# Masked softmax on one core: a contiguous first batch, the last masks moved, batch 14 stored in halves, the first store held longer

The kernel runs on one core of a Trainium2 chip. The metric is device microseconds (us) of that core. Executions are classed as fast or slow by their time and granted clock.

## The reference

For each of 16 batches (8 heads x 256 query rows = 2048 rows of 256 numbers, 2 MB in float32) the first `length` columns of each row go through a softmax; the others are zero.

```python
for b in range(batch):
    length = lengths[b]
    masked = x[b, :, :, :length].copy()
    masked = masked - np.max(masked, axis=-1, keepdims=True)
    exp_masked = np.exp(masked)
    result[b, :, :, :length] = exp_masked / np.sum(exp_masked, axis=-1, keepdims=True)
```

The lengths (128 to 255) are data. A load may stop a little past the length; all of the output must be written.

## The kernel before

A batch is 128 partitions x 16 rows. Eight slots in SBUF hold batches. SyncE loads batches 0 to 3 whole; GpSimd loads the other twelve, with rows cut to one of 11 widths or whole. VectorE masks (a minimum with a falling ramp), ScalarE takes exponentials with their sums half a batch at a time, VectorE divides by halves, and SyncE stores.

```python
x_f = x.rearrange("b h q k -> b (h q) k").rearrange("b (p t) k -> b p t k", p=P)
...
def parts(b):                       # the pieces in which a batch is stored
    if b == 0:
        cuts = [0, nt]
    elif b < 8:
        cuts = [0, half, half + quarter, nt]
    elif b < 13 or b == batch - 1:
        cuts = [0, half, nt]
    else:
        cuts = [0, nt]
...
for h in range(2):
    s = slice(h * half, (h + 1) * half)
    nc.sync.dma_start(out=xt[:, 0, s], in_=x_f[0, :, s]).then_inc(s_ld[h], 16)
for b in range(1, ahead):
    nc.sync.dma_start(out=xt[:, b], in_=x_f[b]).then_inc(s_ld[b + 1], 16)

nc.sync.wait_ge(s_exp, 3)           # the first store is held for three half tiles of ScalarE
for b in range(batch):
    s_b = s_st[b % 2]
    for s in parts(b):
        nc.sync.wait_ge(s_out, 2 * b + (s.stop - 1) // half + 1)
        if b >= 2 and s.start == 0:
            nc.sync.wait_ge(s_b, 64 * (b // 2 + 1))      # the store of batch b - 2 has landed
        nc.sync.dma_start(out=out_f[b, :, s, :], in_=xt[:, b % slots, s, :]).then_inc(s_b, ...)
...
for b in range(batch):              # VectorE
    first = b == 0 or b >= ahead
    if first:
        divide(b, 0)
    if b + 1 < batch:
        mask(b + 1, slice(0, nt))
    if not first:
        divide(b, 0)
    divide(b, 1)
...
with nc.Fori(0, 2 * batch, 1, engines=[ACT]) as i:
    nc.scalar.wait_ge(s_min, i + 1)
    for j in range(half):
        ins = nc.scalar.activation(out=e, in_=e, func=EXP, accum_out=...)
    ins.then_inc(s_exp, 1)
```

The softmax here doesn't subtract the row's maximum and nothing guards it: scores larger than these inputs give would overflow.

Of the kernel before, what the change touches and what calls it, by code (L numbers as in the profile page):

```python
# [20 lines left out]
def kernel(  # L21
# [6 lines left out]
    nc = tc.nc  # L28
    P = nc.NUM_PARTITIONS

    batch, heads, seq_q, seq_k = x.shape
    rows = heads * seq_q
    assert rows % P == 0
    nt = rows // P
    half = nt // 2
    quarter = nt // 4

    x_f = x.rearrange("b h q k -> b (h q) k").rearrange("b (p t) k -> b p t k", p=P)
    out_f = out.rearrange("b h q k -> b (h q) k").rearrange("b (p t) k -> b p t k", p=P)

    slots = 8
    ahead = 4
    assert slots - ahead == 4 and batch % slots == 0
# [6 lines left out]
    def parts(b):  # L50


        if b == 0:
            cuts = [0, nt]
        elif b < 8:
            cuts = [0, half, half + quarter, nt]
        elif b < 13 or b == batch - 1:
            cuts = [0, half, nt]
        else:
            cuts = [0, nt]  # L60
        return [slice(i, j) for i, j in zip(cuts, cuts[1:])]
# [3 lines left out]
    xt = pool.tile([P, slots, nt, seq_k], F32, name="xt")  # L65
# [13 lines left out]
    sem = lambda n: ctx.enter_context(nc.semaphore(n))  # L79
    s_st = [sem("s_st0"), sem("s_st1")]  # L80
    with tc.tile_critical(no_gpsimd_drain=True):  # L81
# [4 lines left out]
        s_ld = [sem(f"s_ld{k}") for k in range(ahead + 1)]  # L86
# [5 lines left out]
        s_v = sem("s_v")  # L92
        s_min = sem("s_min")
        s_exp = sem("s_exp")
        s_out = sem("s_out")

        def length(engine, at):

            return nc.values_load(  # L99
                at,  # L100
                engines=[engine],
                skip_runtime_bounds_check_because="compared with constants, never an address",
            )
# [2 lines left out]
        nc.scalar.dma_start(out=word64, in_=lengths[None, :]).then_inc(s_word, 16)  # L106
        for h in range(2):
            s = slice(h * half, (h + 1) * half)
            nc.sync.dma_start(out=xt[:, 0, s], in_=x_f[0, :, s]).then_inc(s_ld[h], 16)  # L109
        for b in range(1, ahead):  # L110
            nc.sync.dma_start(out=xt[:, b], in_=x_f[b]).then_inc(s_ld[b + 1], 16)  # L111

        nc.sync.wait_ge(s_exp, 3)
        for b in range(batch):
            s_b = s_st[b % 2]
            for s in parts(b):
                nc.sync.wait_ge(s_out, 2 * b + (s.stop - 1) // half + 1)
                if b >= 2 and s.start == 0:
                    nc.sync.wait_ge(s_b, 64 * (b // 2 + 1))
                nc.sync.dma_start(  # L120
                    out=out_f[b, :, s, :], in_=xt[:, b % slots, s, :]
                ).then_inc(s_b, 16 * ((s.stop - s.start) // quarter))



# [44 lines left out]
        def step(ins):  # L170
            nonlocal v
            v += 1
            ins.then_inc(s_v, 1)
# [5 lines left out]
                out=down, in0=iota_i, scalar1=0.5, scalar2=-big, op0=ALU.add, op1=ALU.mult  # L179
# [7 lines left out]
                out=len_s, in0=len_f, scalar1=big, scalar2=None, op0=ALU.mult  # L187
# [4 lines left out]
        def clip(b, s, lo, hi):  # L192

            t = xt[:, b % slots, s, lo:hi]
            return nc.vector.scalar_tensor_tensor(  # L195
                out=t,
                in0=down[:, None, lo:hi].to_broadcast([P, s.stop - s.start, hi - lo]),
                scalar=len_s[:, b : b + 1],
                in1=t,
                op0=ALU.add,  # L200
                op1=ALU.min,
            )

        def mask(b, s):
            v_len = length(DVE, word[0:1, 2 * b : 2 * b + 1])
            if b == 0:
                nc.vector.wait_ge(s_ld[s.start // half], 16)
            elif b < ahead:
                nc.vector.wait_ge(s_ld[b + 1], 16)
            else:  # L210
                nc.vector.wait_ge(s_sw[b % 2], 16 * ((b - ahead) // 2 + 1))
            with nc.vector.If(v_len < mid):  # L212
                clip(b, s, 0, mid)
            clip(b, s, mid, seq_k).then_inc(s_min, (s.stop - s.start) // half)

        def divide(b, h):
            s = slice(h * half, (h + 1) * half)
            nc.vector.wait_ge(s_exp, 2 * b + h + 1)
            step(nc.vector.reciprocal(out=inv_sum[:, b, s], in_=row_sum[:, b, s]))  # L219
            nc.vector.wait_ge(s_v, v)  # L220
            t = xt[:, b % slots, s, :]
            nc.vector.tensor_tensor(  # L222
                out=t,
                in0=t,
                in1=inv_sum[:, b, s, None].to_broadcast([P, half, seq_k]),
                op=ALU.mult,
            ).then_inc(s_out, 1)
# [3 lines left out]
        for b in range(batch):  # L231


            first = b == 0 or b >= ahead
            if first:
                divide(b, 0)
            if b + 1 < batch:
                mask(b + 1, slice(0, nt))
            if not first:
                divide(b, 0)  # L240
            divide(b, 1)


        nc.scalar.activation(out=warm, in_=nc.const_aps.tensor(0.0, (P, 1), F32), func=EXP)  # L244
# [2 lines left out]
        with nc.Fori(0, 2 * batch, 1, engines=[ACT]) as i:  # L247
            nc.scalar.wait_ge(s_min, i + 1)
            at = bass.ds(i % (2 * slots), 1)
            for j in range(half):  # L250
                e = x_h[:, at, j, :]
                ins = nc.scalar.activation(  # L252
                    out=e, in_=e, func=EXP, accum_out=sum_h[:, bass.ds(i, 1), j]
                )
            ins.then_inc(s_exp, 1)


# [33 lines left out]
```

## Time and profile before

| before | value |
|---|---|
| time, median of 6 runs | 156.53 us (155.87 to 156.64) |
| span of the profiled run | 154.7 us |
| VectorE, ScalarE, GpSimd busy | 75%, 68%, 12% |
| DMA | 62.06 MB to and from HBM, 401 GB/s over the span |

A kernel that moves 62 MB at a plateau of some 430 GB/s needs 144 us for that alone. So read the profile for the stretches in which the DMA runs below the plateau. (A packet, below, is what the profile records as one move of a DMA engine, here mostly 4 to 16 KB.) The prediction shows those of the start, of the hand-over from loads to stores, and of the end. What it doesn't show is how the first two loads, the halves of batch 0, landed (the last line of the view of the line that issues them: microseconds from issue to last landing; with two loads, the least is the first half's, the greatest the second's and the median their mean):

```profile
DMA to landing us min/median/max: 5.2/6.2/7.2
```

When the last store was issued (SyncE's timeline: start, length):

```profile
146.65 0.36 SPq L120 DMA_DIRECT2D out_dram<-xt  x1
```

Last, the chain that ended last, by engine:

```profile
DMA 55%; DVE 19%; ACT 8%; issue 8%; ACTq 2%; SPq 1%; POOLq 1%; DVEq 0%
```

The chain ends in VectorE's divides and the last store.

### The profile page before, as it was taken

To read this page: it belongs to the slowest core of one execution; us is meant where nothing else is said; L and a number is where in the kernel's file an instruction comes from. 1 tells how busy PE (TensorE), PEld (TensorE's weight loads), DVE (VectorE), ACT (ScalarE), POOL (GpSimd) and SP (SyncE) were. 2 spreads that over 40 slices of the span, in tenths; PEclk is the share of its full clock that TensorE was granted. 3 is DMA by queue.
4 is the path that set the end of the run, shared out by engine and by line. 5 is a ranking of instruction groups with operands and counts; after the bars stand their busy time and mean duration, and the time that the engine had idled before them with its cause. 6 is when DMAs were issued, how large, how long until landed. Compare 5 with 4: busy or idle time off the path is not lost.

```text
span 154.7 us, 1324 instructions
## 1 busy us (share of the span) xinstructions
PE 0.2 (0%) x1; PEld 0.1 (0%) x1; DVE 115.7 (75%) x84; ACT 105.2 (68%) x514; POOL 19.0 (12%) x25
## 2 busy tenths in 40 slices
PE   0000000000000000000000000000000000000000
PEld 0000000000000000000000000000000000000000
DVE  1249999952999696979979696969689629796700
ACT  3087799992692959778695959595976906959200
POOL 4910031000220110201111020202001000000000
DMA  4999999999999999999999999999999999999992
GB/s 116 426 449 424 428 398 406 398 407 447 400 410 395 402 409 414 415 417 411 404 424 407 417 408 409 415 416 416 416 417 419 419 448 415 426 445 419 430 421 85
DMA packets 9988, 62.08 MB, mean 401 GB/s; under 512 B 850, under 2 KB 946, under 8 KB 6274
## 3 DMA queue, kind: packets, MB, share of 16 engines
q1 hardware_dynamic: 5904, 41.95, 65.8%
q0 software_dynamic: 4080, 20.12, 32.1%
q14 instruction: 2, 0.02, 0.0%
q10 hardware_dynamic: 2, 0.00, 0.0%
HBM read 28.51 MB, written 33.55 MB: 401 GB/s over the span
## 4 chain that ended last, share of the span: by engine, by line
DMA 55%; DVE 19%; ACT 8%; issue 8%; ACTq 2%; SPq 1%; POOLq 1%; DVEq 0%
DMA xt<-in_x_dram 34%; DMA out_dram<-xt 21%; DVE xt L222 9%; DVE xt L195 9%; ACT xt L252 8%; ACTq L252 2%; DVE inv_sum L219 1%; SPq L109 1%; POOLq L99 0%; SPq L111 0%; SPq L120 0%; DVEq L212 0%; POOLq L135 0%; POOLq L130 0%; ACTq L247 0%
## 5 line engine op out<-in xcount | busy, mean ns | idle before, releaser
L252 ACT ACTIVATE xt<-xt x256 | 102.4, 401 | 37.2 <-DVE xt L195 37.2
L222 DVE TENSOR_TENSOR xt<-xt,inv_sum 128x2048 f32<-128x2048 f32 x32 | 73.4, 2292 | 1.1
L252 ACT ACTIVATION_READ_ACCUMULATOR xt<-xt x256 | 47.9, 187 | 0.0
L195 DVE SCALAR_TENSOR_TENSOR xt<-down,len_s,xt 128x2048 f32<-128x2048 f32 (+1 forms) x17 | 37.8, 2222 | 13.1 <-DMA xt<-in_x_dram 13.0
L130 POOL DMA_DIRECT2D xt<-in_x_dram x12 | 12.8, 1064 | 95.5 <-issue 50.6
L219 DVE RECIPROCAL inv_sum<-row_sum 128x8 f32<-128x8 f32 x32 | 6.3, 198 | 14.4 <-ACT xt L252 14.4
L149 POOL MEMSET xt<- 128x1536 f32 x4 | 5.3, 1386 | 1.1 <-DVE len_s L186 1.1
L244 ACT ACT_TABLE_LOAD x1 | 1.3, 1283 | 1.6 <-SPq L81 1.6
L178 DVE TENSOR_SCALAR down<-iota_i 128x256 f32<-128x256 int32 x1 | 0.3, 297 | 1.6 <-POOL iota_i L141 1.6
L183 DVE CAST len_b<-word 1x16 bf16<-1x16 int32 x1 | 0.2, 163 | 0.4 <-DMA word<-in_lengths_dram 0.4
L186 DVE TENSOR_SCALAR len_s<-len_f 128x16 f32<-128x16 f32 x1 | 0.2, 174 | 0.3 <-PE len_f L165 0.3
L141 POOL IOTA iota_i<- 128x256 int32 x1 | 0.3, 331 | 0.6 <-SPq L81 0.6
L146 POOL MEMSET seed<- 1x1 f32 x2 | 0.3, 162 | 0.0
L244 ACT ACTIVATE warm<-const-float32-0.0 128x1 f32<-128x1 f32 x1 | 0.2, 203 | 0.0
L144 POOL MEMSET ones<- 1x128 bf16 x1 | 0.2, 194 | 0.0
L165 PE MATMUL len_f<-len_b,ones 1*128 1x16 bf16 x1 | 0.2, 164 | 2.6 <-DVE len_b L183 2.6
L275 POOL MEMSET const-float32-0.0<- 128x1 f32 x1 | 0.1, 98 | 0.3 <-issue 0.3
L165 PEld LDWEIGHTS len_f<-len_b,ones 1*128 1x128 bf16 x1 | 0.1, 99 | 2.6 <-POOL ones L144 2.6
L275 POOL MEMSET const-float32-1.0<- 128x1 f32 x1 | 0.1, 98 | 0.0
L275 POOL MEMSET const-bfloat16-1.0<- 128x1 bf16 x1 | 0.1, 98 | 0.0
L275 POOL MEMSET const-uint8-127<- 128x1 uint8 x1 | 0.1, 98 | 0.0
L275 POOL BASE_LOAD x1 | 0.0, 17 | 0.1
## 6 DMA issues: line engine op xcount, KB each, us to landing
out_dram<-xt SPq DMA_DIRECT2D x19, 1024.0 KB
out_dram<-xt SPq DMA_DIRECT2D x14, 512.0 KB
xt<-in_x_dram SPq DMA_DIRECT2D x3, 2048.0 KB, 16.1
out_dram<-xt SPq DMA_DIRECT2D x3, 2048.0 KB
xt<-in_x_dram POOLq DMA_DIRECT2D x3, 1728.0 KB, 16.9
xt<-in_x_dram POOLq DMA_DIRECT2D x2, 2048.0 KB, 18.5
xt<-in_x_dram POOLq DMA_DIRECT2D x2, 1600.0 KB, 16.8
xt<-in_x_dram POOLq DMA_DIRECT2D x2, 1280.0 KB, 14.8
```

The lines of the kernel that those rows point to most:

```text
L109: nc.sync.dma_start(out=xt[:, 0, s], in_=x_f[0, :, s]).then_inc(s_ld[h], 16)
L130: nc.gpsimd.dma_start(out=xt[:, slot, :, :w], in_=x_n[:, n, :, :w]).then_inc(s_sw[par], 16)
L141: nc.gpsimd.iota(iota_i, pattern=[[1, seq_k]], base=0, channel_multiplier=0).then_inc(s_iota, 1)
L146: nc.gpsimd.memset(seed[:, par : par + 1], 0.0).then_inc(s_st[par], 64)
L149: nc.gpsimd.memset(xt[:, b, :, low:], 0.0).then_inc(s_fill, 1)
L165: nc.tensor.matmul(len_f, lhsT=ones, rhs=len_b, start=True, stop=True).then_inc(s_lenf, 1)
L195: return nc.vector.scalar_tensor_tensor(out=t, in0=down[:, None, lo:hi].to_broadcast([P, s.stop - s.start, hi - lo]), scalar=len_s[:, b : ...
L219: step(nc.vector.reciprocal(out=inv_sum[:, b, s], in_=row_sum[:, b, s]))
L222: nc.vector.tensor_tensor(out=t, in0=t, in1=inv_sum[:, b, s, None].to_broadcast([P, half, seq_k]), op=ALU.mult,).then_inc(s_out, 1)
L244: nc.scalar.activation(out=warm, in_=nc.const_aps.tensor(0.0, (P, 1), F32), func=EXP)
L252: ins = nc.scalar.activation(out=e, in_=e, func=EXP, accum_out=sum_h[:, bass.ds(i, 1), j])
L275: nc = _bacc.Bacc("TRN2", target_bir_lowering=False, num_devices=1)
```

## The change

The intent as I read it: read the first batch in contiguous halves, so that its first half is there sooner; hold the first store a little longer to keep it out of the way of the last initial load; and at the end bring the masks forward, so that ScalarE gets the last batch sooner and the last stores go out earlier.

```diff
+    x_0 = x[0].rearrange("h q k -> (h q) k").rearrange("(u p t) k -> p u t k", u=2, p=P)
+    out_0 = out[0].rearrange("h q k -> (h q) k").rearrange("(u p t) k -> p u (t k)", u=2, p=P)
...
-        elif b < 13 or b == batch - 1:
+        elif b != batch - 3:
...
-            nc.sync.dma_start(out=xt[:, 0, s], in_=x_f[0, :, s]).then_inc(s_ld[h], 16)
+            nc.sync.dma_start(out=xt[:, 0, s], in_=x_0[:, h]).then_inc(s_ld[h], 16)
...
-        nc.sync.wait_ge(s_exp, 3)
+        nc.sync.wait_ge(s_go, 4)
...
+                if b == 0:
+                    to = out_0
+                    at = xt[:, b, s, :].rearrange("p (u t) k -> p u (t k)", u=2)
+                else: (as before)
...
-            first = b == 0 or b >= ahead
-            if first:
-                divide(b, 0)
-            if b + 1 < batch:
-                mask(b + 1, slice(0, nt))
-            if not first:
-                divide(b, 0)
-            divide(b, 1)
+            at = 0 if b == batch - 2 else 2 if b == batch - 3 else 1 if b == 0 or b >= ahead else 0
+            for h in range(3):
+                if h == at and b + 1 < batch:
+                    mask(b + 1, slice(0, nt))
+                if h < 2:
+                    divide(b, h)
...
+                if j == 1:
+                    ins.then_inc(s_go, 1)
```

`s_go` counts the second activation of each half tile, so the first store now waits until ScalarE is two activations into the fourth half tile, where it waited for the end of the third. On VectorE the order changes only in batches 13 and 14: mask 14 goes behind both divides of 13, mask 15 ahead of both divides of 14.

More of the change, by code (lines that the diff above doesn't have):

```diff
@@ L94 @@
         s_exp = sem("s_exp")
+        s_go = sem("s_go")
         s_out = sem("s_out")
@@ L119 @@
                     nc.sync.wait_ge(s_b, 64 * (b // 2 + 1))
-                nc.sync.dma_start(
-                    out=out_f[b, :, s, :], in_=xt[:, b % slots, s, :]
-                ).then_inc(s_b, 16 * ((s.stop - s.start) // quarter))
+                if b == 0:
+                    to = out_0
+                    at = xt[:, b, s, :].rearrange("p (u t) k -> p u (t k)", u=2)
+                else:
+                    to = out_f[b, :, s, :]
+                    at = xt[:, b % slots, s, :]
+                nc.sync.dma_start(out=to, in_=at).then_inc(s_b, 16 * ((s.stop - s.start) // quarter))
         def pick(v, n, slot, par, ws):
```

## The prediction

> **What bounds the kernel now.** I began with the page: engine shares, the 40 slices and the totals of the DMA.
>
> ```profile
> PE 0.2 (0%) x1; PEld 0.1 (0%) x1; DVE 115.7 (75%) x84; ACT 105.2 (68%) x514; POOL 19.0 (12%) x25
> ...
> DMA  4999999999999999999999999999999999999992
> ```
>
> No compute engine is above 75%, while the DMA row stands at 9 in every slice but the first and the last. So the bytes (28.51 MB read and 33.55 MB written, 62.06 together, which the change leaves as they are) are the bound, and what can be won lies in stretches where the DMA moves less than its full rate. To size these I asked for busy time in short stretches; the last two columns are the DMA share and GB/s (a packet's bytes fall whole into a stretch, so single half-microseconds scatter).
>
> ```profile
> 2.00:2.50 0.50, 0.00 (x0) 0.00 (x0) 0.16 (x1) 0.50 (x1) 0.00 (x0) 1.00 1.18 213
> 2.50:3.00 0.50, 0.16 (x1) 0.10 (x1) 0.17 (x1) 0.49 (x2) 0.00 (x0) 1.00 0.56 147
> 3.00:3.50 0.50, 0.00 (x0) 0.00 (x0) 0.00 (x0) 0.14 (x1) 0.45 (x1) 1.00 0.92 311
> 3.50:4.00 0.50, 0.00 (x0) 0.00 (x0) 0.00 (x0) 0.00 (x0) 0.50 (x1) 1.00 0.84 328
> 4.00:4.50 0.50, 0.00 (x0) 0.00 (x0) 0.00 (x0) 0.00 (x0) 0.50 (x2) 1.00 0.90 360
> ...
> 5.00:20.00 15.00, 0.00 (x0) 0.00 (x0) 10.91 (x8) 9.96 (x49) 3.38 (x3) 1.00 1.02 434
> ```
>
> ```profile
> 21.50:22.00 0.50, 0.00 (x0) 0.00 (x0) 0.50 (x1) 0.50 (x3) 0.50 (x1) 1.00 1.10 360
> 22.00:22.50 0.50, 0.00 (x0) 0.00 (x0) 0.50 (x1) 0.50 (x4) 0.14 (x1) 1.00 0.68 229
> ```
>
> ```profile
> 125.00:151.00 26.00, 0.00 (x0) 0.00 (x0) 16.91 (x12) 12.99 (x64) 0.00 (x0) 1.00 1.01 429
> 151.00:151.50 0.50, 0.00 (x0) 0.00 (x0) 0.00 (x0) 0.00 (x0) 0.00 (x0) 1.00 0.82 344
> 151.50:152.00 0.50, 0.00 (x0) 0.00 (x0) 0.00 (x0) 0.00 (x0) 0.00 (x0) 1.00 0.24 98
> 152.00:152.50 0.50, 0.00 (x0) 0.00 (x0) 0.00 (x0) 0.00 (x0) 0.00 (x0) 1.00 0.19 82
> ```
>
> Full rate is 429 to 434 GB/s. Against it there are four losses. (1) Nothing moves before 2.2 us, and from 2.0 to 4.5 us the five stretches carry 0.5 x (213+147+311+328+360) = 680 KB, 1.57 us of work at 432: 0.9 us lost while the first loads start. The packet records show why: the first 8 KB packets took 0.35 to 1.28 us each, the later ones 0.309. (2) Where the first store follows the four first loads, 21.0 to 24.0 us: the same sum over that stretch (459, 360, 229, 459 for the halves, 377 for the last microsecond) gives 1130 KB, 2.6 us of work, 0.4 us lost; and 26 to 28 us, at 365 GB/s, loses another 0.3 where the first loads from GpSimd's queue set in. (3) In the middle, 45 to 125 us, 413 GB/s with the short rows of the cut loads, which the change does not touch. (4) From 151.0 to 153.0 the engines run out one by one: 270 KB in 2.0 us, so 1.4 us lost to the slowest, then 1.7 us without traffic.
>
> The end is where the order on VectorE matters. Timeline of VectorE (start, length):
>
> ```profile
> 121.00 2.29 DVE L222 TENSOR_TENSOR xt<-xt,inv_sum 128x2048 f32<-128x2048 f32 x1
> 126.58 2.35 DVE L195 SCALAR_TENSOR_TENSOR xt<-down,len_s,xt 128x2048 f32<-128x2048 f32 x1 [3.29 <-DMA xt<-in_x_dram]
> ...
> 134.97 2.34 DVE L195 SCALAR_TENSOR_TENSOR xt<-down,len_s,xt 128x2048 f32<-128x2048 f32 x1
> ...
> 144.33 2.29 DVE L222 TENSOR_TENSOR xt<-xt,inv_sum 128x2048 f32<-128x2048 f32 x1
> ```
>
> Counting back from the end, 144.33 is the second divide of batch 15, 134.97 the mask of 15, 129.08 (cut here) the second divide of 13, and 126.58 the mask of 14, for which VectorE stood idle 3.29 us although it could have divided. That idle time looks like the gain, until SyncE's queue is read:
>
> ```profile
> SPq L119 <- DMA out_dram<-xt: 92.3, 14, 9.7
> ```
>
> Line 119 is the wait for the store two batches back. SyncE issued the store of 13 at 133.81. Its divide had ended at 131.37, but the store of batch 11 had its last landing at 133.75: that landing was the gate.
>
> **What the Trainium skill says.** "DMA: Bandwidth & Descriptors", section "Where 436 GB/s comes from", puts the fabric's ceiling at 435 GB/s, and its note that a core alone reaches nearly that fits here: 429 to 434, so the plateau has no headroom. The same page, section "Queues, rings and completion order", says that each DMA engine takes turns between its queue rows a packet at a time; the trace agrees in that from 28 to 132 us both queues move bytes at once. It follows that a store issued earlier takes turns from a load in flight and does not add bandwidth. In "Latency and other measured facts" the page tells of a slow row pitch at large powers of two, from 512 KiB on; the pitch here is 16 KB, the next loads run at 434 with it, and no trace here shows such a loss. And the page's "Two DMAs through the same engine are not ordered" says that reading and writing sides of an engine are separate queues, so a store behind loads may begin reading while they still write. The slow load packets from 21.0 us on, 1.1 us after the first store was issued at 19.86, would fit that, but GpSimd's first load was issued at 20.85 and would fit too.
>
> **The change part by part.**
>
> Halves of batch 0 contiguous. Each of the 128 rows of a half stays 8 KB, so 128 packets of 0.309 us as before; only the distance between rows in HBM falls from 16 to 8 KB. Were it the pitch that slows the first packets, much of the 0.9 us could come back; but the loads of batches 1 to 3 have the 16 KB pitch and run at the full 434, so a cold start is likelier. I choose a quarter: -0.25 us, and as all 16 engines are busy to the end, what is saved there arrives at the end. The price: the store of batch 0 goes out in 256 packets of 8 KB (0.309 us) in place of 128 of 16 KB (0.611 us): (79.1 - 78.2) / 16 = +0.06 us.
>
> First store held. Now it waits for the third half tile; ScalarE starts the fourth at 19.75, one tile each 0.40 us, so its second activation is done near 20.6. The store is issued at 20.65 in place of 19.86. A queue needs about 1.1 us from issue to first packet (1.13 to 2.2 at the start), so its packets are ready at 21.75. The loads of batch 3 finish their last packets only from 22.5 us on (their landings come at 23.2 to 23.9): the queue does not run dry, with 0.7 us to spare. Of the 0.4 us lost from 21 to 24 I give half to the early store: -0.2 us.
>
> Batch 14 in halves: 256 packets of 8 KB for 128 of 16 KB, again +0.06 us. Its first half can be issued earlier.
>
> Masks ahead of the divides. The second divide of 13 moves from 129.08 to about 124, but its store stays at 133.8 behind the landing of store 11. Mask 14 stays at 126.58, its load's landing. ScalarE then works on 14 from 129.2 to 135.6. Mask 15 waits for its load, whose last landing is at 133.66, so it runs from 133.9 to 136.2 and ScalarE has batch 15 from 136.4 to 142.8 (before: 137.6 to 144.1). The four divides follow the mask, 2.45 us each with the reciprocal: ends at 138.7, 141.1, 143.6, 146.0. So the stores: 14 at 138.75 (gate: landing of store 12 at 138.71) and 141.1, 15 at 143.8 (landing of store 13) and 146.05 in place of 146.65. The last one comes 0.6 us earlier. What is it worth? At 146.65 the DMA still had until 151.2 to run, (151.2 - 146.65) x 0.429 = 1.95 MB, of which the last store is 1.05: 0.9 MB, or 2.1 us of backlog ahead of it. Nothing starves before or after; issuing earlier lengthens the queue. For a little less raggedness at the end I give -0.15 us.
>
> Sum: -0.25 + 0.06 - 0.2 + 0.06 - 0.15 = -0.48 us, on 156.6: 156.1.
>
> **The rivals.** (a) The tail is on the path: the chain of waits runs through the mask of 14, ScalarE and the divides up to 144.33, and the last store is part of it. Were the end tied to the last issue, 0.6 us or more would come off, to 155.6. Against it: 429 GB/s from 125 to 151 and the 2.1 us of backlog. (b) The held store opens a hole: if it takes longer to be ready than 1.1 us (256 pieces in place of 128 to describe), or the loads end earlier than at 22.5, the DMA idles for some tenths: 156.6 to 157.2. GpSimd's first load could not fill it, since its packets come only at 26.5, 5.6 us after its issue. (c) The cold start is wholly pitch and evens the engines: -0.9 us at the start, and part of the 1.4 us raggedness at the end goes with it, since an engine that falls behind in the first microseconds (one 8 KB packet took 1.28 us) has the same work as the others and never catches up: 155.0. For it: the landings of the first half are already 0.5 us apart between the engines. Against: by the end the spread is 2 us, so most of it grows later. (d) Nothing: the start is cold whatever the address, 156.6 with some scatter (the three runs before lie 0.56 us apart).
>
> **Range and chances.** The parts lie within -1.5 and +0.6 us and are not all of one sign; with the scatter of runs I take 155.3 to 156.9. Faster by over 2% would need 3.1 us, more than start, hand-over and ragged end could give if all went well: 3%. Slower by over 2% would need a hole of 3 us in a queue that has backlog everywhere: 2%.
>
> **What would show it.** Right: DMA at 9 in all inner slices, 62.06 MB; more than 272 GB/s on average from 2.0 to 4.5 us; the first store issued near 20.6 and no stretch from 21 to 23 us poorer than before; mask 14 without a divide left over, mask 15 waiting for its load near 134; the last store issued about 146 with the DMA busy 4 to 5 us more. Wrong: a DMA share well under 1 from 21 to 23 us (rival b), traffic that thins out before the last issue (rival a), or a gain of a microsecond already present in the landing of batch 0 (rival c). If the rate in the middle, 413 GB/s, moves by itself, my sum has no term for it.

## The result, and the profile after

| | median | runs | lowest to highest |
|---|---|---|---|
| before | 156.53 us | 6 | 155.87 to 156.64 |
| after | 156.39 us | 6 | 156.27 to 156.56 |

The ratio of after to before is 1.0002, with a 95% interval of 0.9982 to 1.0022: the same. (A ratio here is the mean of one kernel's fast runs over the mean of the other's of the same rounds, so not quite the ratio of the medians.) Nothing was won, nor was anything lost beyond a third of a microsecond.

The page of after, engine shares and the DMA's slices:

```profile
PE 0.2 (0%) x1; PEld 0.1 (0%) x1; DVE 115.7 (75%) x84; ACT 105.2 (68%) x514; POOL 19.0 (12%) x25
...
DMA  3999999999999999999999999999999999999992
```

It is the same picture: the DMA is full in all inner slices. Now the start and the hand-over (where the first store follows the first loads), in the stretches of the prediction (last two columns: DMA share, GB/s):

```profile
2.00:2.50 0.50, 0.00 (x0) 0.00 (x0) 0.16 (x1) 0.50 (x1) 0.00 (x0) 1.00 1.17 131
2.50:3.00 0.50, 0.17 (x1) 0.10 (x1) 0.18 (x1) 0.49 (x2) 0.00 (x0) 1.00 0.31 115
3.00:3.50 0.50, 0.00 (x0) 0.00 (x0) 0.00 (x0) 0.14 (x1) 0.45 (x1) 1.00 0.84 344
3.50:4.00 0.50, 0.00 (x0) 0.00 (x0) 0.00 (x0) 0.00 (x0) 0.50 (x1) 1.00 0.97 410
4.00:4.50 0.50, 0.00 (x0) 0.00 (x0) 0.00 (x0) 0.00 (x0) 0.50 (x2) 1.00 0.98 410
...
21.50:22.00 0.50, 0.00 (x0) 0.00 (x0) 0.50 (x1) 0.50 (x4) 0.34 (x1) 1.00 0.96 360
22.00:22.50 0.50, 0.00 (x0) 0.00 (x0) 0.50 (x1) 0.50 (x3) 0.00 (x0) 1.00 0.56 213
```

From 2.0 to 4.5 us after moved 0.5 x (131+115+344+410+410) = 705 KB, before 680: the first microsecond is poorer, the next is better, and the sum is the same within 25 KB, 0.06 us. The first packets stayed slow with contiguous halves: eight of them took 1.02 to 1.33 us. The stretch from 22.0 to 22.5 us, poorest before with 229 GB/s, is still the poorest, with 213. Both loads land 0.3 us earlier:

```profile
DMA to landing us min/median/max: 4.9/5.9/6.9
```

Coarser stretches are more telling for the hand-over. Before:

```profile
20.00:24.00 4.00, 0.00 (x0) 0.00 (x0) 3.93 (x5) 4.00 (x21) 1.29 (x1) 1.00 1.00 389
24.00:28.00 4.00, 0.00 (x0) 0.00 (x0) 4.00 (x2) 4.00 (x21) 0.56 (x1) 1.00 0.97 389
```

and after:

```profile
20.00:24.00 4.00, 0.00 (x0) 0.00 (x0) 3.93 (x5) 4.00 (x21) 1.86 (x2) 1.00 0.98 406
24.00:28.00 4.00, 0.00 (x0) 0.00 (x0) 4.00 (x3) 4.00 (x21) 0.00 (x0) 1.00 1.00 372
```

After gains 4 x (406 - 389) = 68 KB in the first four microseconds and loses 4 x (389 - 372) = 68 KB in the next four. The gain is there, and is given back at once.

The end of after, first VectorE's timeline (L231 is the divide, L204 the mask), then SyncE's wait for the store two batches back, SyncE's last issue, and the stretches:

```profile
125.00 2.29 DVE L231 TENSOR_TENSOR xt<-xt,inv_sum 128x2048 f32<-128x2048 f32 x1
127.38 2.35 DVE L204 SCALAR_TENSOR_TENSOR xt<-down,len_s,xt 128x2048 f32<-128x2048 f32 x1
134.68 2.35 DVE L204 SCALAR_TENSOR_TENSOR xt<-down,len_s,xt 128x2048 f32<-128x2048 f32 x1 [4.96 <-DMA xt<-in_x_dram]
...
144.50 2.29 DVE L231 TENSOR_TENSOR xt<-xt,inv_sum 128x2048 f32<-128x2048 f32 x1
```

```profile
SPq L124 <- DMA out_dram<-xt: 88.8, 14, 9.9
```

```profile
146.82 0.37 SPq L131 DMA_DIRECT2D out_dram<-xt  x1
```

```profile
125.00:151.00 26.00, 0.00 (x0) 0.00 (x0) 16.62 (x11) 12.98 (x64) 0.00 (x0) 1.00 1.01 429
151.00:151.50 0.50, 0.00 (x0) 0.00 (x0) 0.00 (x0) 0.00 (x0) 0.00 (x0) 1.00 1.00 426
151.50:152.00 0.50, 0.00 (x0) 0.00 (x0) 0.00 (x0) 0.00 (x0) 0.00 (x0) 1.00 0.59 246
```

The idle 3.29 us before mask 14 are gone, but VectorE now waits 4.96 us for the load of batch 15. The second divide of 13 starts at 125.00 in place of 129.08, yet the store of 13 was issued at 134.00 (before: 133.81), because the store of 11 had landed at 133.94. The last store goes out at 146.82, 0.17 us later than before; the load of batch 15, which the mask of 15 waits for, had its last landing at 134.45 (before: 133.66). The DMA moves 429 GB/s from 125 to 151 us in both kernels.

### The profile page after: what moved, and what is told of

It is laid out like the page before. It is cut to its first block, busy times and chain, and to the rows that moved or that the text cites. A ratio compares the mean times of both kernels' runs of the same rounds, so it can differ in the third digit from the quotient of the medians.

```text
span 154.8 us, 1325 instructions
## 1 busy us (share of the span) xinstructions
PE 0.2 (0%) x1; PEld 0.1 (0%) x1; DVE 115.7 (75%) x84; ACT 105.2 (68%) x514; POOL 19.0 (12%) x25
## 3 DMA queue, kind: packets, MB, share of 16 engines
q1 hardware_dynamic: 6176, 41.95, 65.8%
HBM read 28.51 MB, written 33.55 MB: 401 GB/s over the span
## 4 chain that ended last, share of the span: by engine, by line
DMA 66%; DVE 19%; issue 4%; SPq 2%; ACT 1%; POOLq 1%; ACTq 0%; DVEq 0%
DMA xt<-in_x_dram 45%; DMA out_dram<-xt 21%; DVE xt L231 13%; DVE xt L204 6%; ACT xt L260 1%; SPq L131 1%; DVE inv_sum L228 1%; SPq L114 1%; ACTq L260 0%; POOLq L139 0%; SPq L116 0%; POOLq L144 0%; DVEq L221 0%; POOLq L166 0%; POOLq L146 0%
## 5 line engine op out<-in xcount | busy, mean ns | idle before, releaser
L231 DVE TENSOR_TENSOR xt<-xt,inv_sum 128x2048 f32<-128x2048 f32 x32 | 73.4, 2292 | 1.1
L204 DVE SCALAR_TENSOR_TENSOR xt<-down,len_s,xt 128x2048 f32<-128x2048 f32 (+1 forms) x17 | 37.8, 2223 | 15.5 <-DMA xt<-in_x_dram 15.3
```

Of the source, the lines that this page charges most:

```text
L204: return nc.vector.scalar_tensor_tensor(out=t, in0=down[:, None, lo:hi].to_broadcast([P, s.stop - s.start, hi - lo]), scalar=len_s[:, b : ...
L231: nc.vector.tensor_tensor(out=t, in0=t, in1=inv_sum[:, b, s, None].to_broadcast([P, half, seq_k]), op=ALU.mult,).then_inc(s_out, 1)
```

## The experiments

Twelve kernels ran in three groups (no e4 ran), each beside runs of the kernel before on the same chip. The diffs are against before unless it says after.

| label | median us (runs) | before us (runs) | ratio | 95% interval |
|---|---|---|---|---|
| e0_before_again | 156.08 (6) | 156.22 (11) | 1.0003 | 0.9978 to 1.0029 |
| e1_contiguous_alone | 156.01 (6) | 156.22 (11) | 0.9992 | 0.9970 to 1.0014 |
| e2_hold_alone | 156.17 (5) | 156.22 (11) | 0.9998 | 0.9976 to 1.0021 |
| e3_tail_alone | 156.13 (6) | 156.22 (11) | 1.0001 | 0.9980 to 1.0023 |
| e5_no_hold | 156.34 (4) | 156.03 (11) | 1.0029 | 1.0005 to 1.0052 |
| e6_hold_gpsimd_later | 156.72 (4) | 156.03 (11) | 1.0039 | 1.0018 to 1.0059 |
| e7_small_gpsimd_load_first | 156.74 (6) | 156.03 (11) | 1.0045 | 1.0020 to 1.0069 |
| e8_stores_in_halves | 160.07 (5) | 156.03 (11) | 1.0255 | 1.0236 to 1.0273 |
| e9_last_divide_2us_later | 156.12 (6) | 156.08 (11) | 1.0001 | 0.9989 to 1.0014 |
| e10_last_divide_5us_later | 157.53 (4) | 156.08 (11) | 1.0060 | 1.0012 to 1.0108 |
| e11_small_store_early | 156.90 (6) | 156.08 (11) | 1.0047 | 1.0031 to 1.0063 |
| e12_before_stores_in_halves | 159.86 (4) | 156.08 (11) | 1.0228 | 1.0209 to 1.0247 |

All gave correct results. None beats before and after; e1, the lowest, lies within its interval of 1.

### The parts one by one: e0, e1, e2, e3

e0 is the kernel before with a comment. e1 takes only the lines with `x_0` and `out_0`, e2 only those with `s_go`, e3 only those of `parts` and of VectorE's order.

> The kernel before, unchanged, as a control. It sets what counts as noise: time within 0.3% of before (ratio 0.997 to 1.003). In the trace the stretches used below should repeat to about 5 GB/s: some 375 GB/s from 20 to 24 us falling short of 430, the loss of 26 to 28 us (365), full rate from 125 to 151. If a second profile of the same kernel differs from the first by as much as after differs from before in these stretches, then no stretch can be laid to the change.

> Only the contiguous halves of batch 0 (loads, and its store in 8 KB pieces). Theory A (a gain at the start and the hand-over is given back by the 8 KB store): the last landing of the first half at 6.0 us in place of 6.3, a poorer stretch from 24 to 28 us (about 370 GB/s against 390 before), time within 0.2% of before. Rival B (the loss at 26 to 28 us comes from holding the store): 24 to 28 us as before, and 0.3 us faster.

> Only the hold; the store of batch 0 keeps 16 KB pieces. Theory A: the hand-over, 20.5 to 24 us, gains 0.2 us, 24 to 28 us stay as before, so 0.2 us faster at most, 156.3. Rival B: 24 to 28 us fall to about 370 GB/s and nothing is won. Rival C (no hold matters, the hand-over is cold writes): 20.5 to 24 us as poor as before.

> Only the order of the last masks and batch 14 in halves. My theory: the DMA has backlog at every one of the last issues, so no change, ratio 0.999 to 1.001, though VectorE waits some 5 us for the load of batch 15 and the last store is issued within 0.6 us of before. Rival (the tail is on the path, as the chain of waits has it): 0.5 us or more faster, or slower by as much if the mask of 15 now holds the divides of 14 too long.

All four are the same in time. The control failed its own condition, and that is worth knowing: a second profile of the same kernel gives other values in the very stretches that I had read the change from.

```profile
20.00:24.00 4.00, 0.00 (x0) 0.00 (x0) 3.93 (x5) 4.00 (x22) 1.43 (x2) 1.00 1.01 365
24.00:28.00 4.00, 0.00 (x0) 0.00 (x0) 4.00 (x2) 4.00 (x22) 0.42 (x1) 1.00 0.99 416
```

That is e0; the first profile of before had 389 and 389. So one profile of before against one of after doesn't settle the hand-over, and theory A, that the 8 KB pieces of the first store give the gain back, can't be read from it. e1 speaks against it: with those pieces and without the hold, 24 to 28 us are at 413 GB/s. e2, which has the hold and 16 KB pieces, shows the opposite:

```profile
20.00:24.00 4.00, 0.00 (x0) 0.00 (x0) 3.93 (x5) 4.00 (x22) 1.73 (x2) 1.00 1.02 434
24.00:28.00 4.00, 0.00 (x0) 0.00 (x0) 4.00 (x2) 4.00 (x22) 0.12 (x1) 1.00 0.95 355
```

So the hold is what moves the loss (the table below has all profiles): rival B of e2 in the main, with a hand-over that became perfect (434) paid for from 24 to 28 us (355) and from 40 to 43 us (344). As for the contiguous halves, the first half's last landing in e1 is at 5.99 us, as expected, against 6.34 in the first profile of before and 6.14 in the control. All 14 profiles agree: 5.92 to 6.05 us in the five with contiguous halves, 6.12 to 6.40 in the nine without. But from 2 to 5 us e1 moved 300 GB/s, before 300 and e0 309. The engines were evened out, not sped up: the first half's landings on the 16 engines lie between 5.67 and 5.99 us in e1, between 5.43 and 6.34 in before. e3 has the last store at 146.36 (146.65 and 145.87 in the two profiles of before) with VectorE idle 4.95 us before mask 15: my theory of the tail held.

### Where the loss at the hand-over goes: e5, e6, e7, e11

```diff
 e5: -        nc.sync.wait_ge(s_exp, 3)
 e6: (e2 and)
     -        nc.gpsimd.wait_ge(s_ld[ahead - 1], 16)
     +        nc.gpsimd.wait_ge(s_ld[ahead], 16)
 e7: (against after)
     +        nc.gpsimd.dma_start(out=first, in_=x_f[batch - 1, :, 0, 0:8]).then_inc(s_first, 16)
     +        nc.gpsimd.wait_ge(s_first, 16)
 e11: (against after)
     +        nc.scalar.wait_ge(s_ld[0], 16)
     +        nc.scalar.dma_start(out=out_f[batch - 1, :, 0, 0:128], in_=zero).then_inc(s_early, 16)
     ...
     +        nc.sync.wait_ge(s_early, 16)
```

> The kernel before without any hold: the first store goes out when its divide is done, near 18.8 us, a microsecond earlier. Theory A (a fixed loss where stores and GpSimd's loads set in, some 0.7 us between 20 and 43 us, which the hold only moves): 20 to 24 us at 375 GB/s or less, 24 to 28 us at 405 or more, 40 to 43 us at 390 or more, time within 0.2% of before. Rival B (the earlier the store, the more is lost): 0.3 us or more slower, and the loss of 20 to 43 us summed grows beyond 1 us.

> Hold alone, with GpSimd's first load also held until batch 3 has landed, so issued near 25.5 us in place of 20.8. Theory A1 (the loss at 24 to 28 us belongs to the first packets of GpSimd's queue): 24 to 28 us back at 415 GB/s or more, and the loss comes some 5 us later, at 30 to 34 us. Theory A2 (it belongs to the first store, whose slow packets only come later with the hold): 24 to 28 us stay at 355 to 372. Time within 0.3% of before in both.

> The kernel after, with a 4 KB load (128 pieces of 32 B) on GpSimd's queue near 8.5 us, before its first real load. If the loss at 24 to 28 us is a cold start of that queue, it goes: 24 to 28 us at 410 GB/s or more and 0.2 to 0.4 us faster. If it lies in reads and writes meeting there, nothing changes: 24 to 28 us at 372 as in after, time within 0.1%.

> The kernel after, with a 64 KB store on ScalarE's queue near 6.5 us, in the middle of the first loads, into rows that the last store overwrites. Theory D (the loss of 0.6 to 1 us is paid once, when writes first meet reads, wherever that is): it comes at 7 to 10 us, and 24 to 28 us and 40 to 43 us go up to 410 GB/s or more; time within 0.2% of after, or 0.3 us faster if a small meeting is cheaper. Rival (it belongs to the volume of store and load that meet): 24 to 28 us stay at 372, 5 to 20 us at 430, time as after.

The table puts the runs in the order in which their first store was issued (SyncE's timeline), with GB/s by stretch. "Lost" is worked out from the row: the shortfall of each stretch against 430, times its length, summed and divided by 430. (e9 and e10 come further down; but for one idle VectorE instruction their start is that of before, so they are two more profiles of it. e8 and e12, with other store pieces, are left out.)

| run | first store | 20 to 24 | 24 to 28 | 28 to 40 | 40 to 43 | lost us |
|---|---|---|---|---|---|---|
| e5 | 18.70 us | 320 | 424 | 416 | 421 | 1.5 |
| e1 | 19.52 | 356 | 413 | 424 | 413 | 1.1 |
| e9 | 19.67 | 356 | 403 | 426 | 389 | 1.3 |
| e0 | 19.68 | 365 | 416 | 424 | 388 | 1.2 |
| e10 | 19.76 | 369 | 412 | 423 | 389 | 1.2 |
| e3 | 19.82 | 373 | 408 | 425 | 388 | 1.2 |
| before | 19.86 | 389 | 389 | 428 | 389 | 1.1 |
| after | 20.35 | 406 | 372 | 423 | 388 | 1.3 |
| e7 | 20.38 | 406 | 373 | 424 | 388 | 1.2 |
| e11 | 20.51 | 416 | 374 | 429 | 371 | 1.1 |
| e2 | 20.57 | 434 | 355 | 427 | 344 | 1.3 |
| e6 | 20.73 | 430 | 410 | 385 | 434 | 1.4 |

The column from 20 to 24 us rises with the time of the first store almost without exception, and that from 24 to 28 falls in the main, e6 apart. The sum stays at 1.1 to 1.3 us over the whole range of first stores from 19.5 to 20.6 us; taking the hold away altogether makes it 1.5, and the time 0.3% longer. That an early store is worse is not quite shown by it: e5's profiled run was the fastest of its four, at 156.06 us. A hold beyond that of before buys nothing. Between before and after it is a loss that moves, not one that goes. The four profiles with the start of before (e9, e0, e10, before) differ in the same sense; but e3, within 0.04 us of before, is 16 GB/s below it from 20 to 24, so the time of issue isn't the whole of it.

In e6 GpSimd's first load is issued at 26.42 in place of about 20.7 us, and most of the loss goes with it, as theory A1 has it. (The time didn't stay within the expected 0.3%: e6 is 0.39% slower.) The stretch in which that load's packets begin (31 us in the packet records), in e6:

```profile
30.50:34.00 3.50, 0.00 (x0) 0.00 (x0) 2.73 (x3) 3.50 (x19) 0.00 (x0) 1.00 1.03 306
```

and in after:

```profile
30.50:34.00 3.50, 0.00 (x0) 0.00 (x0) 2.38 (x2) 3.50 (x19) 0.00 (x0) 1.00 1.01 413
```

In e2, from which e6 differs by this wait alone, it was at 412 GB/s. From 20 to 28 us, with the first stores but no GpSimd load, e6 lost only 0.2 us. So the first store alone is not what costs; with the longer hold the loss sits where the loads of GpSimd's queue first run beside stores. (With the shorter holds it sits from 20 to 24 us, where SyncE's own last load ends and GpSimd's queue has no packet yet.)

Two explanations were then tried and fell. A cold queue of GpSimd's: e7 ran a small load on it at 8.32 us and the loss stayed (373 from 24 to 28). A price paid once, when the first write meets reads: e11 issued a store of 64 KB at 6.13 us, its packets ran amid the loads (9.6 to 13.8 us), no loss showed there (434 from 5 to 20 us, as before), and 24 to 28 us stayed at 374. What is left, that it takes the meeting of a bulk of stores with a bulk of loads, fits all the rows, but no run isolates it: the cause inside the DMA stays open.

What the packet records add is that the loss is slow packets more than idle engines: in before the 16 KB packets of SyncE's queue took 611 ns each from 19 to 20 us and 733 on average from 21 to 22, in e6 the 4 KB ones 318 from 31 to 32 in place of 162. The 0.5% by which e7 and e11 are slower stays open too. e7's profiled run, at 156.47 us, was no slower than after's at 156.44, so its trace can't show it; e11's, its slowest, moved 409 GB/s from 43 to 125 us and 423 from 125 to 150.5, where after had 412 and 428: some 0.9 us, so its loss lies late, not at the hand-over.

### The backlog at the end: e9, e10

```diff
+            if b == batch - 1:
+                for _ in range(1):      # e10: range(2)
+                    nc.vector.wait_ge(s_v, v)
+                    step(nc.vector.tensor_tensor(out=idle, in0=idle, in1=idle, op=ALU.mult))
             divide(b, 1)
```

> The kernel before, with one idle VectorE multiply of 2.3 us ahead of the very last divide, so the last store is issued near 148.3 in place of 146.65 us. Theory (backlog): that store's packets are ready at 149.4; on an average engine the queue ahead of it runs dry at 151.2 - 2.44 = 148.8, on the slowest engine, which sets the end, at about 150.3. So the end moves by 0 to 0.6 us, nearer 0. Rival (the chain of waits is right that the last divide sets the end): 1.65 us longer.

> The same with two idle multiplies, the last store near 150.6 us, its packets ready at 151.7. Theory: now both are dry; every engine begins the last store at 151.7 and needs 2.44 us, so bytes end at 154.1 in place of 152.75 on the slowest: 1.4 us longer, at most 3. Rival (the last divide sets the end): 3.95 us longer.

e9's last store was issued at 149.13 (I had expected 148.3), 2.5 us later than before, and the time is the same, ratio 1.0001. Its end in stretches:

```profile
149.00:150.00 1.00, 0.00 (x0) 0.00 (x0) 0.10 (x1) 0.00 (x0) 0.00 (x0) 1.00 0.34 139
150.00:151.00 1.00, 0.00 (x0) 0.00 (x0) 0.00 (x0) 0.00 (x0) 0.00 (x0) 1.00 1.04 434
151.00:152.00 1.00, 0.00 (x0) 0.00 (x0) 0.00 (x0) 0.00 (x0) 0.00 (x0) 1.00 1.03 418
152.00:153.00 1.00, 0.00 (x0) 0.00 (x0) 0.00 (x0) 0.00 (x0) 0.00 (x0) 1.00 0.36 148
```

Most DMA engines ran dry for a moment at 149 to 150, and that cost nothing: two to three of the 16, by the packet records, still had work, and the slowest sets the end. The last store then landed on all 16 engines between 152.82 and 153.21 us; in before its landings were spread from 151.53 to 153.51, so only the early ones were delayed. e10's last store, at 151.24, comes after all have run dry:

```profile
150.00:151.00 1.00, 0.00 (x0) 0.00 (x0) 1.00 (x1) 0.00 (x0) 0.00 (x0) 1.00 0.00 0
151.00:152.00 1.00, 0.00 (x0) 0.00 (x0) 0.21 (x1) 0.00 (x0) 0.00 (x0) 1.00 0.00 0
152.00:153.00 1.00, 0.00 (x0) 0.00 (x0) 0.00 (x0) 0.00 (x0) 0.00 (x0) 1.00 0.93 393
```

Its span is 156.3 us, 1.6 longer than before (1.4 expected). The four runs scatter from 155.90 to 158.22, and the lowest shows no loss at all; no trace of it was kept. The slack, by how much the last store may be late at no cost, is thus at least 2.5 us (e9), and by the one profile of e10 4.6 - 1.6 = 3.0, worked out, not measured. The rival, that the last divide sets the end, would have had 2.5 us in e9 by the times as they fell.

### The size of the store pieces: e8, e12

```diff
-        elif b < 8:
-            cuts = [0, half, half + quarter, nt]
```

e8 does this to after, e12 to before.

> The kernel after, with the stores of batches 1 to 7 in two halves in place of a half and two quarters, so no packet of 4 KB. In the trace 4 KB packets took 162 ns and 8 KB 315, so 1792 x 162 / 16 = 18.1 us of all engines become 896 x 315 / 16 = 17.6: 0.5 us faster if the bound is DMA time as I hold, 155.9. Rival (the quarters are there because the later store is issued later, and the pause costs more): same or slower.

> The kernel before with the stores of batches 1 to 7 in halves, as e8 was with after. Theory: the 8 KB packets give the stores a larger share than 4 KB ones when the two queues take turns, the loads fall behind, and the DMA runs out of stores near 142 us while the last batch is still in work: 3 us slower or more, as e8. What the order of the last masks is worth shows only here: in e8 mask 15 waited for its load with the divides of 14 behind it; in the order of before the first divide of 14 comes first but its whole-batch store waits for the second. I expect e12 within 1 us of e8, either way.

I was wrong on e8 by its sign: 2.55% slower, not 0.5 us faster. The slices of its page, and SyncE's longest wait:

```profile
DMA  4999999999999999999999999999999999990995
```

```profile
SPq L129 <- DVE xt L229: 93.8, 26, 7.8
```

```profile
142.00:146.00 4.00, 0.00 (x0) 0.00 (x0) 3.93 (x5) 4.00 (x21) 0.00 (x0) 1.00 0.15 61
```

There is a hole of four microseconds at 142 us. SyncE no longer waits for old stores but for VectorE: the stores have caught up with the computing. The reason is in the packet records. From 45 to 80 us loads moved 185 GB/s and stores 223 in after; in e8 it was 151 and 264, in e12 153 and 261. A store packet of 8 KB took 316 ns, one of 4 KB 163, while the counts of load and store packets stayed near one to one (1485 and 1463 in after, 1208 and 1130 in e8): if the engines take turns by packets, as these counts suggest, the loads get less. The edit leaves the times of issue alone, as both quarters waited for the same divide. The loads fell behind: the last load was issued at 124.15 us, in after at 116.86. At 142 us all issued stores were done, and batches 14 and 15 were still in work. e12 has the same hole (82 GB/s from 142 to 146 us) and is 2.28% slower: their ratios lie 0.3% apart with intervals that overlap, so the whole change, the order of the last masks with it, is worth little even where no backlog hides it.

## Why the prediction was right or wrong

The class and the range held (156.39 in 155.3 to 156.9). The point of 156.1 claimed a gain of 0.48 us, 0.3%; the interval of the ratio ends at 0.9982, a gain of 0.28 us. The gain was not there, and rival (d), nothing, came true. The range held because it had room for nothing as well as for a gain; that is no merit of the sum.

- **Bound.** Right. The DMA row stays at 9 in after, and from 45 us on the stretches repeat (413 and 412 GB/s in the middle).
- **Halves contiguous, -0.25 us.** Mis-sized: about 0. The bytes moved from 2.0 to 4.5 us differ by 0.06 us' worth, the slowest landing of the first half came 0.1 to 0.3 us earlier, and e1 is the same in time. "What is saved there arrives at the end" did not hold: an even start is no gain in bytes. My sign of more than 272 GB/s from 2.0 to 4.5 us was met (282) and shows nothing, as e0, without the change, had 278. The argument against the pitch was the better one, and the quarter that I gave it was not earned.
- **Hold, -0.2 us.** This is the step that failed. "Of the 0.4 us lost from 21 to 24 I give half to the early store" took the loss for one that an overlap causes in place, the store taking turns with the load in flight. But the turns that I reckoned with are between queues, and SyncE's loads and stores are in one (q1 of the page: 41.95 MB, 33.55 of them stores). In after the first store's 8 KB packets begin at 22.37 us, as the load's last 16 KB packets end, and run at full speed (309 to 316 ns up to 23 us bar one of 333); the slow packets (up to 895 ns for 611) are the load's, ahead of them. (That load's landings began at 22.84 us in before, not at 23.2; nothing hangs on it.) The runs show a loss of 1.1 to 1.3 us between 20 and 43 us that a later store pushes from 20 to 24 us into 24 to 28 and, in e2, 40 to 43. The hand-over did get better, from 389 to 406 GB/s; I had no term for where it would come back. No hole opened (rival b): the store was issued at 20.35 against 20.65 estimated, and in e2, issued later still, the hand-over ran at 434.
- **Two times +0.06 us for 8 KB pieces.** Too small to be tested, as the control's interval alone reaches some 0.4 us to either side.
- **Order at the end, -0.15 us.** The mechanism was right: the gates were the landings of older stores and of the load of batch 15 (mask 15 at 134.68, estimated 133.9), and the backlog covers the rest. The size was wrong by its sign: the last store came 0.17 us later, not 0.6 earlier. The load of batch 15 landed 0.79 us later than in the profile that I reckoned from, and 134.45 plus my own steps gives 146.84; in e0, the same kernel as before, that landing was at 132.92, so one profile can't time a last store to 0.6 us. e3 and e9 show that neither matters, since the slack is at least 2.5 us; my 2.1 was for the average engine and left the slowest out.
- **Rival (a)**, the chain of waits as the bound, fell with e9: its divide was 2.5 us later, at no cost.
- **Rival (c)**, a start that evens the engines: the first half's landings were indeed closer together in after, 0.36 us apart for 0.91 in before (not 0.5, as I had read them), but the ragged end stayed: the last store's landings are 1.64 us apart in e1, 1.70 in e0, and the bytes of the last stretch only moved (344 to 426 GB/s from 151.0 to 151.5, with the end where it was).

## What to carry to other kernels

While the DMA is full from start to end and stays so, moving an issue or a mask changes who waits but hardly when the bytes are done; before giving a reordering any time, count the backlog in front of the last store, and delay that store on purpose to measure its slack. A loss seen in one stretch is saved only if the sum over the neighbouring stretches falls too, and one profile of each kernel can't show that: take a second of the old one first. The size of store pieces also sets the shares of two queues, so coarser pieces may starve the loads that the end depends on.

## What the Trainium skill lacked or had wrong

- "DMA: Bandwidth & Descriptors", "Rules for kernel authors", advises at least 1 MiB for each DMA for bandwidth. No run here contradicts that, but here 1 MiB stores in place of 0.5 MiB ones for the second halves of seven batches cost 2.3 to 2.6% (e12, e8). Its section "Queues, rings and completion order" tells of the turns by packets, but not what follows: larger store packets took load bandwidth (185 to 151 GB/s).
- The same page, "Latency and other measured facts", gives about 1 us from a GpSimd issue to the first byte. With SyncE's queue busy, the first load's packets began 5.6 us after its issue in before (20.85 to 26.47), and 3.8 us in e7 for a small load (8.32 to 12.13). No run here has an issue from GpSimd with the other queue idle.
- No page has the loss of 1.1 to 1.5 us of DMA time in the 23 us in which stores and GpSimd's loads set in beside each other, nor that it moves with their order.
- No page has a figure for how far apart the engines end behind a long queue: the last store's landings were spread over 2 us (151.5 to 153.5 in before), so that the average engine's backlog (2.1 us) understates the slack (3.0).
